# x in transposed layout, the first products taken ahead of the norm with its factor put on their results, and dt kept on chip

## The chip, the cores and the metric

The kernel runs on one core of a Trainium2 chip. That core has five engines, each with an instruction queue of its own: PE (TensorE, matrix products), DVE (VectorE), ACT (ScalarE), POOL (GpSimd) and SP (SyncE, which here only issues DMAs; ACT issues some too). On chip there are SBUF (128 partitions) and PSUM (eight banks, into which PE writes). The metric is device time in microseconds (us), the median of several executions.

## The reference, cut to what matters

One layer, 512 tokens, d_model 2048, float32 throughout:

```python
h = rmsnorm(x, norm_w)              # x * rsqrt(mean(x*x) + 1e-6) * norm_w
u = h @ w_in                        # one input projection, its columns split into
z_ssm, xbc, dt_f, dt_b, q_a, kv_a, z_attn, g_ssm, g_attn = split(u)
xbc = silu(dwconv(xbc) + bias)      # depthwise, four taps along the tokens
dt = softplus(dt + dt_bias)         # per head and direction
y = ssd(xs, dt, A, B, C) + flip(ssd(flip ...)) + d_skip * xs     # four groups
y = group_rmsnorm(y * silu(z_ssm))
o = mla(q_a, kv_a) * silu(z_attn)   # 16 heads
x + ((y @ w_proj_ssm) * sigmoid(g_ssm) + (o @ w_proj_attn) * sigmoid(g_attn)) @ w_out
```

followed by a last rmsnorm. The norm's root, r = rsqrt(mean(x*x) + 1e-6), is one number per token, so (x * norm_w) @ w, multiplied by r token by token, is h @ w.

## The kernel before

**Precision.** Every large product is made of three matmuls: each operand is split into a high part (rounded to the type fp32r) and a low part (what the rounding left), and `mm3` (L167) issues high x high, high x low, low x high for one k-block of 128. One such group of three is a *step* here. A product of a 128-column weight tile with all 512 tokens has 16 steps (D = 16 k-blocks). Weights come from DRAM in halves of 8 k-blocks: `wchunk` (L157) loads one half (SP issues it), ACT casts it to its high part, DVE subtracts for the low part (tile names wraw, wh, wl, three buffers each).

**Order.** PE's order is the program's. DVE, ACT, POOL and SP are ordered by a scheduler that takes ready work by priority; weights are requested ahead of their place (`ahead`, `tc.high_priority`). Each engine then runs its queue strictly in order.

**Start (L198 to L243).** x lies in DRAM with tokens in rows. It is loaded in 8 pieces (`xt`, [128 tokens, 1024]). ACT squares each piece and sums it over the row; the root per token comes from a few one-column instructions on DVE (`small_rsqrt`, L183); DVE (or ACT) multiplies the rows by it; PE turns all of it with 64 transposes (`x_turn`, L225) into eight PSUM banks; `x_out` (L227) multiplies by norm_w and splits, into h_h on ACT and h_l on DVE. Only then does the first product start.

**First products.** In this order: dt (64 rows of dt and 64 of the rotary key, `dtp`); then, for SSD group 0, the tiles xbc 4 and 5 (B and C) and xbc 0 to 3 (`xbc_gen`: the product, `conv_silu` on DVE and ACT, result to DRAM as `xbc_d`). Between them `h_sums` (L705) adds h_h and h_l together again and forms sums and differences of quarters of h (S1 to S4), the operands of the Strassen products; S1, S2, S4 stay in SBUF, x21 and S3 go to DRAM. `dt_make` (L278) computes softplus as a polynomial on DVE and writes dt and dt * A to DRAM (`dt_d`, `da_d`).

**Gates.** Three products of 2048 x 2048 (`wz`, `wgs`, `wga`) with the tokens, each by Strassen's scheme in two column halves cp; a half is seven products P1, P5, P6, P2, P3, P7, P4 (`Strassen.pair`, L630). Weight sums are made by a second load that adds into the first (`w_more`) or on POOL and DVE. Functions may be hung behind a product of a half (`hooks`).

**SSD.** Group 0 begins with `dt_turn` (L305; four transposes of dt64, which was loaded back from `dt_d` at L815) and `dt_sums` (L313; running sums of dt * A by four 128x128 matmuls); then BT and CT (L890, L891, xbc 4 and 5 from DRAM), xs (L894), and so on through four groups. Attention and the last products follow.

The few lines that the steps below rest on:

```python
def mm3(out, wh, wl, xh, xl, start, stop):
    pe.matmul(out, wh, xh, start=start, stop=False)
    pe.matmul(out, wh, xl, start=False, stop=False)
    pe.matmul(out, wl, xh, start=False, stop=stop)
```

## Time and profile before

| | us |
|---|---|
| median of 3 runs | 2069.7 (2066.1 to 2075.88) |
| profiled execution, its own time | 2068.9 |
| profiled execution, span | 2066.8 |

The page shows busy time of each engine, the span in 40 slices, the DMA queues and the chain of waits. A row of the trace reads: start and duration in us, engine, line, operation, out<-in by the program's names, sizes; in square brackets the idle time of the engine ahead of it and what ended that. A row of the windows reads: the stretch and its length, then busy us and count for PE, PE's weight load, DVE, ACT, POOL, then the granted clock of PE as a share of full speed, the DMA engines' busy share, and GB/s. In grouped rows the number after the bar is the group's busy time, then the mean ns of one. What the rows show is told in the prediction, where they are used.

### The profile page before, as it was taken

Reading aid. Unit: us, or ns where it says so; the run is one execution under the profiler, and the core shown is the slowest. Engines: PE = TensorE matmul, PEld = TensorE weight load, DVE = VectorE, ACT = ScalarE, POOL = GpSimd, SP = SyncE. Lnnn points to the kernel's source line nnn. Section 1 sums busy time; section 2 is a strip of 40 time slices with the busy share of each in tenths; the row PEclk is TensorE's granted clock in tenths of the full one; section 3 lists DMA queues with packets and bytes.
Section 4 is the critical chain, followed back from the end, with each engine's and each line's share of the span. In section 5 each row is a group of like instructions: output and inputs, shape, how many; then the busy total and the mean of one; then the engine's idle time right before and its main releaser. Section 6 shows DMA issues by size and latency. Waiting matters only on the chain.

```text
span 2066.8 us, 24703 instructions
## 1 busy us (share of the span) xinstructions
PE 1970.5 (95%) x9074; PEld 1627.3 (79%) x9074; DVE 1463.1 (71%) x1946; ACT 959.3 (46%) x1344; POOL 315.9 (15%) x337
## 2 busy tenths in 40 slices
PE   6999999999989999899899999999998999999998
PEld 5888888888867877787788788788877787888886
DVE  7976676676659689788786666667576888776342
ACT  6444444444444545445555344444444444443232
POOL 0011010010042151332420001110010111100110
PEclk9999999999999999999999999999999999999999
DMA  5567657656556837677564857873376876865332
GB/s 195 168 173 197 182 121 187 194 124 171 144 171 186 243 120 191 225 211 219 166 182 150 240 166 185 217 199 96 85 213 251 294 245 250 268 227 168 104 120 82
DMA packets 166584, 378.56 MB, mean 183 GB/s; under 512 B 16000, under 2 KB 65280, under 8 KB 165888
## 3 DMA queue, kind: packets, MB, share of 16 engines
q1 hardware_dynamic: 104688, 238.33, 35.2%
q0 software_dynamic: 26944, 92.29, 20.5%
q10 hardware_dynamic: 34832, 46.38, 6.3%
q8 instruction: 71, 1.16, 0.2%
q14 instruction: 49, 0.40, 0.1%
HBM read 325.03 MB, written 98.04 MB: 205 GB/s over the span
## 4 chain that ended last, share of the span: by engine, by line
PE 69%; DVE 11%; DMA 9%; issue 6%; ACT 2%; POOL 1%; SPq 0%; ACTq 0%; DVEq 0%; POOLq 0%
PE P L563 10%; PE P L564 10%; PE P L562 10%; PE f L1485 3%; PE f L1486 3%; PE f L1484 3%; PE za L168 2%; PE za L169 2%; PE za L170 2%; PE xbc L168 2%; PE xbc L169 2%; PE xbc L170 2%; DVE wl L164 2%; DVE sum L995 1%; DMA wraw<-wps 1%
## 5 line engine op out<-in xcount | busy, mean ns | idle before, releaser
L433 DVE TENSOR_TENSOR wl<-X,wh 128x1024 fp32r<-128x1024 f32 x152 | 185.2, 1222 | 81.8 <-ACT wh L432 81.3
L432 ACT CAST wh<-X 128x1024 fp32r<-128x1024 f32 x152 | 159.6, 1053 | 160.0 <-PE P L564 134.6
L164 DVE TENSOR_TENSOR wl<-wraw,wh 128x1024 fp32r<-128x1024 f32 (+2 forms) x148 | 175.4, 1186 | 81.7 <-ACT wh L163 76.4
L163 ACT CAST wh<-wraw 128x1024 fp32r<-128x1024 f32 (+2 forms) x150 | 145.3, 969 | 157.4 <-PE xbc L169 43.5
L433 DVE TENSOR_TENSOR wl<-wraw,wh 128x1024 fp32r<-128x1024 f32 x74 | 91.3, 1233 | 98.5 <-ACT wh L432 98.3
L168 PE MATMUL xbc<-h_h,wh 128*128 128x512 f32 x384 | 151.8, 395 | 0.0
L170 PE MATMUL xbc<-h_h,wl 128*128 128x512 f32 x384 | 150.2, 391 | 0.1
L169 PE MATMUL xbc<-h_l,wh 128*128 128x512 f32 x384 | 150.0, 391 | 0.0
L433 DVE TENSOR_TENSOR wl<-Y,wh 128x1024 fp32r<-128x1024 f32 x80 | 97.8, 1223 | 73.1 <-ACT wh L432 73.0
L563 PE MATMUL P<-wl,h_h 128*128 128x512 f32 x384 | 149.4, 389 | 0.0
L564 PE MATMUL P<-wh,h_l 128*128 128x512 f32 x384 | 149.4, 389 | 0.0
L562 PE MATMUL P<-wh,h_h 128*128 128x512 f32 x384 | 149.4, 389 | 0.0
L432 ACT CAST wh<-wraw 128x1024 fp32r<-128x1024 f32 x74 | 78.0, 1054 | 146.0 <-PE f L1486 71.0
L432 ACT CAST wh<-Y 128x1024 fp32r<-128x1024 f32 x80 | 84.2, 1053 | 114.8 <-PE P L564 95.3
L563 PE MATMUL P<-wl,S 128*128 128x512 f32 x288 | 112.4, 390 | 0.6 <-DVE wl L433 0.6
L564 PE MATMUL P<-wh,S 128*128 128x512 f32 x288 | 112.1, 389 | 0.0
L562 PE MATMUL P<-wh,S 128*128 128x512 f32 x288 | 112.1, 389 | 0.0
L170 PE MATMUL za<-h_h,wl 128*128 128x512 f32 x256 | 101.2, 395 | 5.0 <-DVE wl L164 5.0
L168 PE MATMUL za<-h_h,wh 128*128 128x512 f32 x256 | 102.3, 400 | 0.0
L169 PE MATMUL za<-h_l,wh 128*128 128x512 f32 x256 | 100.6, 393 | 0.0
L170 PEld LDWEIGHTS xbc<-h_h,wl 128*128 128x128 f32 x384 | 72.3, 188 | 16.1 <-DVE small L841 0.6
L168 PEld LDWEIGHTS xbc<-h_h,wh 128*128 128x128 f32 x384 | 72.6, 189 | 15.0 <-issue 0.2
(634 smaller groups left out, 5189.0 us busy)
## 6 DMA issues: line engine op xcount, KB each, us to landing
wraw<-wi SPq DMA_DIRECT2D x102, 512.0 KB, 4.1
da<-da_d SPq DMA_DIRECT2D x64, 256.0 KB, 4.4
T_wps<-wps POOLq DMA_DIRECT2D x32, 512.0 KB, 6.2
T_wpa<-wpa POOLq DMA_DIRECT2D x32, 512.0 KB, 9.9
wraw<-wo SPq DMA_DIRECT2D x32, 512.0 KB, 3.4
wraw<-wps SPq DMA_DIRECT2D x24, 512.0 KB, 5.0
xbc_d<-xbc ACTq DMA_DIRECT2D x24, 256.0 KB, 2.9
wraw<-wun SPq DMA_DIRECT2D x16, 384.0 KB, 3.1
```

Source lines behind the costliest of these rows:

```text
L163: act.copy(h, raw)
L164: (dve if ahead[0] else pool).tensor_sub(l, raw, h.bitcast(F32))
L168: pe.matmul(out, wh, xh, start=start, stop=False)
L169: pe.matmul(out, wh, xl, start=False, stop=False)
L170: pe.matmul(out, wl, xh, start=False, stop=stop)
L432: act.copy(hi_, raw)
L433: dve.tensor_sub(lo_, raw, hi_.bitcast(F32))
L562: pe.matmul(bs[i], xh, wh, start=(j == 0), stop=False)
L563: pe.matmul(bs[i], xh, wl, start=False, stop=False)
L564: pe.matmul(bs[i], xl, wh, start=False, stop=(j == 7))
L1484: pe.matmul(acc, mh, wh, start=(start and k == 0), stop=False)
L1485: pe.matmul(acc, mh, wl, start=False, stop=False)
```

## The change

**x comes transposed.** The host gives x a second time as `xt`, with the model dimension on the partitions: 8 pieces of [128, 1024], two k-blocks each. PE's 64 transposes go. SP loads the first halves of the weights of dt, xbc 4 and xbc 5 between the pieces. For each piece ACT squares it (`sq`), DVE multiplies it by norm_w (`x_t`, kept), and `x_split` makes h_h and h_l of it: the operands lack the root.

**Sums of squares** are now over the partitions: `square_sums(j)` takes the piece's squares as the stationary operand against one column of ones, 8 matmuls of one column for a piece, into four PSUM banks `ss`. `factor` makes the root of it (four tokens' columns at once), spreads it over a diagonal (`dg`), and four matmuls with ones give the root as a row for all partitions, which ACT copies to `R` [128, 512].

**Three products run at once.** dt, xbc 4 and xbc 5 are taken step by step in turns as `order` lists them (A, B, C), on operands without the root; the sums of squares stand after every second step and the factor after step 17. Their results are then multiplied by R. Meanwhile DVE multiplies x_t by R and splits it again, so that all that follows has h as before. xbc 0 and 1 run in turns too. `h_sums` takes its quarters from x_t, without adding h_h and h_l; it stands ahead of xbc 2 and xbc 3.

**dt.** The product's result (with bias) goes to DRAM (`dv_d`) and back; `dt_make` is hung behind P5 of the first gate's second half; dt64 stays in SBUF and `dt_d` is gone.

**The first gate** has its P1 and P2 of both halves taken ahead (`head`, `head_end`), as another product of the program had; its weight sums are made by second loads (16 more of 512 KB) and xbc 3 no longer stands between its first columns and its products.

The core of the diff:

```diff
+    for j in range(8):
+        xs = x_t[:, 2 * j:2 * j + 2, :].rearrange("p k t -> p (k t)")
+        nc.sync.dma_start(xs, a["xt"][j])
+        if j in (0, 1, 3):
+            early.append(wchunk(a["wi"][(T_DT, T_XBC + 4, T_XBC + 5)[len(early)], 0], 1024))
+        squares.append(sxq("sq"))
+        act.activation(squares[j], xs, AF.Square)
+        for k in (2 * j, 2 * j + 1):
+            dve.tensor_scalar_mul(x_t[:, k, :], x_t[:, k, :], vec[:, V_NORM + k:V_NORM + k + 1])
+            x_split(k)
...
+    def square_sums(j):
+        for k in range(2):
+            for t in range(TT):
+                pe.matmul(ss[t][:, 0:1], squares[j][:, k * SEQ + t * P:k * SEQ + (t + 1) * P], ones[:, 0:1],
+                          start=(j + k == 0), stop=(j == 7 and k == 1))
+    def factor():
+        v4 = few(4)
         for t in range(TT):
+            dve.tensor_scalar(v4[:, t:t + 1], ss[t][:, 0:1], 1.0 / D, EPS, ALU.mult, ALU.add)
+        r4 = small_rsqrt(v4, 4, lambda n: few(4))
+        dg = sx.tile([P, SEQ], F32, tag="v", bufs=1, name="dg")
+        for t in range(TT):
+            dve.tensor_scalar_mul(dg[:, t * P:(t + 1) * P], ident, r4[:, t:t + 1])
+        rp = pc("rp")
+        for t in range(TT):
+            pe.matmul(rp[:, t * P:(t + 1) * P], ones, dg[:, t * P:(t + 1) * P], start=True, stop=True)
+        act.copy(R, rp)
...
-        put(dt_d, dt64)
...
-        def columns(self, t, cp, m):
+        def columns(self, t, cp, m, headed):
             if self.made:
                 return t_load(t, self.w, cp, "T1", m)
-            return w_load(t, self.w, cp, 0, 0, m)
+            w_load(t, self.w, cp, 0, 0, m)
+            if headed:
+                w_more(t, self.w, cp, 0, 1, m, LOAD_AHEAD)
+            return t
...
+    order = "AABABABC" + "ABC" * 3 + "A" + "BCBC" + "ACAC" + "BABAC" + "ABC" * 3 + "A" + "BCBCBCC"
+    square_sums(0)
+    square_sums(1)
+    for i in together([gemm_steps(p_, win(t), h_h, h_l, w_) for p_, t, w_ in zip(firsts, (T_DT, T_XBC + 4, T_XBC + 5), early)], order):
+        if i % 2 == 1 and i // 2 < 6:
+            square_sums(2 + i // 2)
+        if i == 16:
+            factor()
+    v_ = sx.tile([P, SEQ], F32, tag="v", bufs=1, name="dt_v")
+    dve.tensor_mul(v_, firsts[0], R)
...
+    for k in range(KT):
+        dve.tensor_mul(x_t[:, k, :], x_t[:, k, :], R)
+        x_split(k)
+        if k in (1, 3):
+            xbc_done(4 + k // 2, firsts[1 + k // 2])
+    for i in together([xbc_gen(0, i, None) for i in (0, 1)], "AAA" + "AB" * 13 + "BBB"):
+        pass
+    for i in (2, 3):
+        h_sums(i - 2)
+        run(xbc_gen(0, i, None))
...
+    gates[0].hooks = {(0, "P5"): [lambda: h_ops.load("S3"), lambda: [h_part("S3", 256, q) for q in range(2)]],
+                      (1, "P5"): [dt_make]}
...
-    gates[0].first_columns(0)
-    run(xbc_gen(0, 3, None))
-    for p_ in gates:
+    run(gates[0].head())
+    run(gates[0].pair(0, True))
+    run(gates[0].head_end())
+    run(gates[0].pair(1, True))
+    for p_ in gates[1:]:
...
-    dt64 = tmp2("dt64")
-    with tc.high_priority(offset=LOAD_AHEAD):
-        nc.sync.dma_start(dt64, dt_d)
```

Three places of the instruction queues follow. In the rows, a name left of the arrow is the tile written, "x3" counts like instructions in a run.

PE's first instructions; before, the transposes (mm, pa, pb, pc are the eight banks, xt_239 and xt_256 two blocks of 128 tokens):

```order
L225 MATMUL mm<-cst,xt_239 128x128 x3
L225 MATMUL pa<-cst,xt_239 128x128 x2
L225 MATMUL pb<-cst,xt_239 128x128 x2
L225 MATMUL pc<-cst,xt_239 128x128
L225 MATMUL mm<-cst,xt_256 128x128 x3
```

and now, PE's first instructions, the sums of squares (ss) and the first two steps of the dt product:

```order
L236 MATMUL ss<-cst,sq 128x1 x16
L168 MATMUL dtp<-h_h,wh 128x512
L169 MATMUL dtp<-h_l,wh 128x512
L170 MATMUL dtp<-h_h,wl 128x512
L168 MATMUL dtp<-h_h,wh 128x512
L169 MATMUL dtp<-h_l,wh 128x512
L170 MATMUL dtp<-h_h,wl 128x512
L236 MATMUL ss<-cst,sq 128x1 x8
L168 MATMUL xbc<-h_h,wh 128x512
```

The products thus stand among the sums of squares at the head of the queue, and each waits for its own k-block alone.

DVE around the factor, now: the last scalings and subtractions of x (x_t, h_l), the root (small), the diagonal (dg), and then the first k-blocks times R:

```order
L228 TENSOR_SCALAR x_t<-x_t,vec 128x512 x5
L216 TENSOR_TENSOR h_l<-x_t,h_h 128x512 x5
L243 TENSOR_SCALAR small<-ss 128x1 x4
L187 RECIPROCAL small<-small 128x4
L188 TENSOR_TENSOR small<-small 128x4
L189 TENSOR_TENSOR small<-small 128x4
L190 TENSOR_SCALAR small<-small 128x4
L191 TENSOR_TENSOR small<-small 128x4
L247 TENSOR_SCALAR dg<-cst,small 128x128 x4
L753 TENSOR_TENSOR x_t<-x_t,R 128x512 x2
L164 TENSOR_TENSOR wl<-wraw,wh 128x1024
L216 TENSOR_TENSOR h_l<-x_t,h_h 128x512 x2
```

Before, the root stood there four times, once for each block of tokens, between scalings of rows; it stands there once now, behind all of x, and x's multiplication by R and second split come behind it.

SP where the gates end and the SSD begins; before, with dt's load ahead of BT and CT:

```order
L160 DMA wraw<-wi 128x1024 x3
L768 DMA Y<-h_x_199 128x1024 x2
L160 DMA wraw<-wi 128x1024 x3
L815 DMA dt_4305<-dt_d 128x512
L890 DMA BT<-xbc_d_4_97 128x512
L891 DMA CT<-xbc_d_5_98 128x512
L894 DMA xs<-xbc_d_0_93 128x512
```

and now:

```order
L160 DMA wraw<-wi 128x1024 x3
L794 DMA Y<-h_x_198 128x1024 x2
L160 DMA wraw<-wi 128x1024 x3
L916 DMA BT<-xbc_d_4_97 128x512
L917 DMA CT<-xbc_d_5_98 128x512
L920 DMA xs<-xbc_d_0_93 128x512
L920 DMA xs<-xbc_d_1_94 128x512
```

The load of dt has gone from the queue and nothing else at that place has moved.

More of the change, by code (lines that the diff above doesn't have):

```diff
@@ new lines, in build @@
+    squares, early = [], []
+    ahead[0] = 1
+    for j in range(8):
[8 more added lines that the diff above has]
+            x_split(k)
@@ L264, in build @@
-    for _ in range(5):
-        sxq("first")
-    def put(dst, t):
-        act.dma_start(dst, t)
-    dtp = in_gemm(T_DT, "dtp")
     ahead[0] = AHEAD
     da_d = dr.tile([64, SEQ], F32, name="da_d")
-    dv_, dt64 = sxd("dv_"), sxd("dt64")
-    act.activation(dv_[0:64, :], dtp[0:64, :], AF.Identity, bias=vec[0:64, V_DTB:V_DTB + 1])
-    act.copy(dv_[64:128, :], dtp[64:128, :])
-    put(kr_d, dv_[64:128, :])
-    def dt_make(new):
-        v = dv_[0:64, :]
-        e, u, pl, da64 = (new(n)[0:64, :] for n in ("e", "u", "pl", "da64"))
+    dv_d = dr.tile([64, SEQ], F32, name="dv_d")
@@ L367, in run, with gemm_steps @@
             pass
-    def gemm_steps(out, chunks, xh, xl):
+    def gemm_steps(out, chunks, xh, xl, first=None):
         total = sum(c[2] for c in chunks)
         for src, k0, nk in chunks:
-            h, l = wchunk(src, nk * P)
+            h, l = first if first and k0 == 0 else wchunk(src, nk * P)
             for k in range(nk):
@@ L626, in head, with head_end @@
             self.p1 = (a, b)
[L627 removed]
+        def head_end(self):
+            return self.second(1, self.p1[1], lambda i: sum_tile("p5"), None, "P2b")
         def pair(self, cp, headed=False):
@@ L730, in h_sums @@
-        keep("S4", x12)
-    for i in range(5):
-        run(xbc_gen(0, (4, 5, 0, 1, 2, 3)[i], sxt))
-        if i in (1, 3):
-            h_sums(i // 2)
-    dt_make(sxd)
+        s1, s3 = sxq("s1"), sxq("s3")
+        put(view4(h_d["x21"][:, cs]), x(1, 0))
+        dve.tensor_sub(view4(s1), x(1, 0), x(1, 1))
+        keep("S1", s1)
+        dve.tensor_sub(view4(s3), x(0, 0), x(1, 0))
+        put(h_d["S3"][:, cs], s3)
+        s2 = sxq("s2")
+        dve.tensor_sub(view4(s2), view4(s1), x(0, 0))
@@ new lines, in h_sums, with together, xbc_done @@
+        keep("S2", s2)
+        dve.tensor_add(view4(s1), view4(s2), x(0, 1))
+        keep("S4", s1)
+    def together(gens, order):
+        gens = {n: g_ for n, g_ in zip("ABC", gens)}
+        for i, n in enumerate(order):
+            next(gens[n])
+            yield i
+        for g_ in gens.values():
+            run(g_)
+    def xbc_done(i, p_):
+        v_ = sx.tile([P, SEQ], F32, tag="v", bufs=1, name="xbc_v")
+        dve.tensor_mul(v_, p_, R)
+        o = st("xbc")
+        put(xbc_d[0][i], conv_silu(v_, (4 + 12, 4 + 16)[i - 4], o, lambda n: o))
@@ new lines, in build @@
+    firsts = [mm(n) for n in ("dtp", "xbc", "xbc")]
+    order = "AABABABC" + "ABC" * 3 + "A" + "BCBC" + "ACAC" + "BABAC" + "ABC" * 3 + "A" + "BCBCBCC"
+    assert all(order.count(n) == KT for n in "ABC")
+    square_sums(0)
[5 more added lines that the diff above has]
+            factor()
```

118 lines of the change are left out of this document (43 added, 75 removed).

## Prediction, made before the changed kernel ran

> **What bounds the kernel now.** I read the page first: shares of busy time, the slices, the chain of waits.
>
> ```profile
> span 2066.8 us, 24703 instructions
> PE 1970.5 (95%) x9074; PEld 1627.3 (79%) x9074; DVE 1463.1 (71%) x1946; ACT 959.3 (46%) x1344; POOL 315.9 (15%) x337
> PE   6999999999989999899899999999998999999998
> PE 69%; DVE 11%; DMA 9%; issue 6%; ACT 2%; POOL 1%; SPq 0%; ACTq 0%; DVEq 0%; POOLq 0%
> ```
>
> PE is the bound, busy 95% of the span; only some 96 us can be won by waiting less. The first slice (a 6) is one of the few weak ones. Next, busy time by stretches up to the end of the gate products, and who PE waited for, here (the last of these rows is for 36 to 300 us alone):
>
> ```profile
> 0.00:36.00 36.00, 16.66 (x79) 13.54 (x80) 22.40 (x50) 25.39 (x43) 4.99 (x8) 1.00 0.54 203
> 36.00:300.00 264.00, 263.44 (x1160) 217.17 (x1159) 202.28 (x204) 123.78 (x139) 17.44 (x20) 1.00 0.61 168
> 300.00:566.00 266.00, 266.00 (x1175) 220.30 (x1174) 179.61 (x175) 128.71 (x143) 24.19 (x28) 1.00 0.63 164
> ...
> PE mm L225 <- DVE xt L220: 19.3, 4, 11.1
> PE pb L308 <- DMA dt<-dt_d: 5.4, 1, 5.4
> PE P L563 <- DVE wl L433: 0.6, 2, 0.3
> ```
>
> The first number after the stretch's length is PE's busy time. From 36 to 566 us PE stands still for 0.56 us in all. So the change can win in three places only: before the first product, those 0.6 us, and the 5.4 us on dt. The start, row by row on PE:
>
> ```profile
> 11.07 0.90 PE L225 MATMUL mm<-cst,xt 128*128 128x128 f32 x3 [11.07 <-DVE xt L220]
> ...
> 25.17 0.90 PE L225 MATMUL mm<-cst,xt 128*128 128x128 f32 x3 [6.30 <-DVE xt L220]
> ...
> 27.21 2.43 PE L225 MATMUL mm<-cst,xt 128*128 128x128 f32 x12
> 29.48 1.04 PE L225 MATMUL pa<-cst,xt 128*128 128x128 f32 x8
> ...
> 32.47 0.50 PE L168 MATMUL dtp<-h_h,wh 128*128 128x512 f32 x1
> ...
> 65.02 0.39 PE L170 MATMUL xbc<-h_h,wl 128*128 128x512 f32 x1
> 65.25 0.39 PE L168 MATMUL xbc<-h_h,wh 128*128 128x512 f32 x1
> ```
>
> The first product begins at 32.47; the first three (dt, xbc 4, xbc 5: 144 matmuls) end at 65.25, so a matmul takes 32.78 / 144 = 0.2276 us and a step of one product (three matmuls) 0.683 us. **65.25 is the mark that the new start has to beat.**
>
> **The change, part by part. 1: the start.** Removed are 64 transposes and the wait for the norm; PE now gets, while x comes in, 17 steps of the three products, 64 matmuls of one column (sums of squares) and the four of the factor; the other 31 steps follow it. When each can start is in these rows:
>
> ```profile
> 5.87 1.06 ACT L210 ACTIVATE scr<-xt 128x1024 f32<-128x1024 f32 x1 [2.71 <-DMA xt<-x]
> 7.50 1.06 ACT L210 ACTIVATE scr<-xt 128x1024 f32<-128x1024 f32 x1 [0.48 <-DMA xt<-x]
> 7.73 0.17 DVE L820 TENSOR_SCALAR small<-vec 128x8 f32<-128x8 f32 x1 [7.73 <-DMA vec<-vec]
> 8.68 0.16 DVE L212 TENSOR_TENSOR small<-small 128x1 f32<-128x1 f32 x1 [0.78 <-ACT scr L210]
> ...
> 10.07 0.16 DVE L191 TENSOR_TENSOR small<-small 128x1 f32<-128x1 f32 x1
> ...
> GB/s 0 33 195 280 309 394 426 393 418 422 410 430 414 422 422 414 426 401 37 0 0 0 90 262 209 250 238 0 0 0 0 0 0 0 16 0 0 0 82 356
> ...
> 75.25 0.41 DVE L286 TENSOR_SCALAR u<-e 64x512 f32<-64x512 f32 x1
> L595 DVE TENSOR_TENSOR u<-u,P 128x512 f32<-128x512 f32 x12 | 7.7, 680 | 0.0
> L433 DVE TENSOR_TENSOR wl<-wraw,wh 128x1024 fp32r<-128x1024 f32 x74 | 91.3, 1233 | 98.5 <-ACT wh L432 98.3
> L931 ACT CAST xw_h<-xw 128x512 fp32r<-128x512 f32 x24 | 14.8, 618 | 9.7 <-POOL xw L928 7.9 <-PE off L169 1.6 <-ACT y L851 0.2
> ```
>
> The first transfer was there at 5.87 and the second at 7.50; now a weight chunk is first and x's first piece second, so the first square ends near 8.5. The transfers (GB/s, 1 us a slice) move 0.41 MB a us: x (4.2 MB), three weight chunks (1.6) and the constants (0.5) are down by about 18 us, as the same bytes were before, and hide behind what follows. DVE, from 7.9: 16 scalings by norm_w at 0.41 (the row has 64 partitions; I take 512 elements to cost the same on 128), 16 subtractions at 0.68, three weight splits at 1.23 = 21.1, to 29.0. ACT, from 5.9: 8 squares at 1.06, 16 casts at 0.62, three of weights at 1.06 like the squares = 21.6, to 27.5, waits aside. The factor then costs DVE nine small instructions and four of 128x128 and ACT one root, some 3.2 us (the seven small ones and a root of before took from 8.68 to 10.23), and PE 0.9: **33.1 us by DVE**.
>
> By PE's queue it depends on the one-column matmul, which no row shows. The nearest, and what the clock does:
>
> ```profile
> 1126.96 1.00 PE L1016 MATMUL yb<-xT,G 128*128 128x64 f32 x8
> L1016 PE MATMUL yb<-xT,G 128*128 128x64 f32 x256 | 33.7, 277 | 1.0 <-DVE y L1019 1.0
> 576.85 1.12 PE L308 MATMUL pb<-cst,dt 128*128 128x128 f32 x4 [5.41 <-DMA dt<-dt_d]
> L308 PE MATMUL pb<-cst,dt 128*128 128x128 f32 x4 | 1.1, 436 | 5.4 <-DMA dt<-dt_d 5.4
> ...
> 574.00:578.00 4.00, 1.12 (x4) 0.72 (x4) 0.00 (x0) 0.00 (x0) 0.00 (x0) 0.66 0.78 272
> 578.00:582.00 4.00, 3.29 (x13) 3.01 (x14) 0.49 (x2) 3.41 (x6) 1.80 (x2) 0.50 1.08 379
> 582.00:586.00 4.00, 3.03 (x22) 2.44 (x21) 0.69 (x1) 2.67 (x6) 0.00 (x0) 0.99 0.77 263
> ```
>
> A true f32 matmul is two records: four matmuls of 64 columns are the eight of the first row, and with the last one's 0.277 taken off one begins every (1.00 - 0.277) / 7 = 0.104 us. Two passes of 64 columns, at a dense matmul's pace of 0.2276 / 4 for 128, are 0.057 of it, so about 0.047 is left for loading weights: a record of one column costs between 0.047 and 0.104. I take 0.07, about the middle. PE, from 8.5: 17 x 0.683 = 11.6, 128 x 0.07 = 9.0, eight of the factor 0.9; to 30.0. The clock column (third from the end) tells the rest: after a stall it fell to 0.50 for nearly 7 us and came back some 5 us into new work. At the start, too, 12 transposes took 2.43 us and the next ones, at 29.48, half of that each. So PE begins at half speed; 5 us of that cost 2.5, and the wait for the second square 1.1: **33.6 us by PE**, a near tie. With the tie not quite free I take 33.8; then 31 x 0.683 = 21.2: the three products end at 55.0. **Term 1: -10.2** (-11.5 with the best overlap on DVE, -5.9 with records at 0.104).
>
> On the clock, the Trainium skill ("TensorE: Matmul & The Clock Gate", Part 1) says that about 3.4 us of sustained matmul activity open it and an idle window of that length closes it; the rows above agree in size. Its Part 4 says that transposes don't count as such work. By that, the old start would have met its products cold; the halved transposes at 29.48 speak against it here. Whether one-column matmuls count is the first rival.
>
> **2: the same products' results, and x times the factor.** ACT's copy of R waits for PE, and behind it in ACT's queue stand the second weight halves, for which PE comes 3.4 us later: cast 1.05 and split 1.23 behind two multiplications, about 2.4 us after R, which fits. Then DVE multiplies x by R and splits it again (32 x 0.68 = 21.8), 11 weight splits (13.5), 18 convolution steps (13.2), the operand sums (8 x 1.23) and their splits (6 x 1.23), three results (2.0): 67.7 us, against 21.2 + 4 x 10.9 = 64.9 of PE until the next stage. DVE is full, as it was (a convolution step's row, and 30 to 105 us):
>
> ```profile
> L388 DVE SCALAR_TENSOR_TENSOR cacc<-xbc,vec,cacc 128x510 f32<-128x510 f32 x23 | 16.8, 732 | 0.0
> ...
> 30.00:105.00 75.00, 75.00 (x337) 61.61 (x336) 71.41 (x82) 38.67 (x48) 0.00 (x0) 1.00 0.50 161
> ```
>
> There DVE was 95% busy and PE lost nothing; what is late may slip into the four products after it, which need DVE for four splits (4.9 us) in 10.9. The tight point is the second weight half of xbc 1, behind S1's difference and the late splits of x. **Term 2: +1.5** (0 to +4).
>
> **3: dt on chip.** PE's 5.4 us on dt go; late next are BT and CT, which were in the same queue right behind:
>
> ```profile
> CT<-xbc_d SPq DMA_DIRECT2D x1, 256.0 KB, 7.4
> ...
> 578.59 0.62 ACT L895 CAST c_h<-CT 128x512 fp32r<-128x512 f32 x1
> ...
> 585.54 0.59 ACT L883 COPY xT<-pb 128x512 f32<-128x512 f32 x1 [0.26 <-PE pb L872]
> ...
> 586.20 2.04 POOL L928 TENSOR_TENSOR xw<-xT,wst 128x512 f32<-128x512 f32 x2 [5.10 <-ACT xT L883]
> ```
>
> CT was down at about 578.5; one 256 KB transfer fewer ahead puts it at 578.0. From there ACT does in order c_h 0.62, a table load 1.28, two exponentials, b_h and four xT, about 5.5 us: 583.5 in place of 586.1, and POOL's xw, on which PE's next product waits, follows. **Term 3: -2.6** (0 to -4.4). The dt arithmetic goes into the first gate's second half; it issues one load on SP, behind S3's two, and two writes on ACT, read 400 us later; in 36 to 300 us DVE is 77% busy.
>
> **4: the first gate's head.** Same seven products a half; 16 more loads of 512 KB (8.4 MB) in some 150 us, 56 GB/s on top of 168 at a DMA share of 0.61. POOL's accumulations now come four products early; they covered the 0.6 us. **Term 4: -0.6** (0 to -0.6). From the second gate on, each engine's order is as before but for dt's load.
>
> Sum: -10.2 + 1.5 - 2.6 - 0.6 = -11.9. The profiled execution took 2068.9 (2066.8 of span), 0.8 below the median of the runs shown; **2057.0**. The likeliest case alone spans 2053 to 2061.
>
> **The rivals.** *The clock stays half* (slower): if PE's short, load-heavy work doesn't open it, the stage to the factor runs at the half-clock price. At dt's row (four in 1.12 us, one every (1.12 - 0.436) / 3 = 0.228): 8.5 + 128 x 0.228 + 17 x 1.366 + 8 x 0.228 = 62.7, then 21.2 + 2.5: 86.4, or 21.2 late: 2068.9 + 21.2 + 1.5 - 3.2 = 2088. At half that price, 0.114, 2074. A us at half clock costs half a us: it decides if the clock opens later than about 37 us, 24 us after the time I allow. For it: waits between short matmuls. Against: transposes, half load, opened it. 0.12, half of it beyond 0.5%.
>
> *Dear weight loads*: a record at 0.104, as in the 64-column row, adds 128 x 0.034 = 4.4: 2061. 0.13. The same page ("LDWEIGHTS") gives columns / 1.2 ns, 107 ns for 128; with its floor of 25 ns an estimate of 0.132 a record, 7.9 us more, 2065. The trace speaks against that: 0.104 a record with the 64 columns in it.
>
> *DVE bounds the second stage*: 4 to 6 us at the tight point, 2061. 0.10. For it: 67.7 against 64.9.
>
> *It doesn't get ahead*: squares, scalings, casts and subtractions of a piece hand over between ACT and DVE; wholly in series a piece takes 4.5 us, the weights 6.9 in all, and the three products end 10 us past the mark (2077); half so, 2067. Both queues take two pieces in turn, which speaks against. 0.05.
>
> **The numbers.** 0.60 for the forecast. The range 2052 to 2066 leaves out the half clock, the last rival and a little below: 0.2. 0.5% (10.3 us) is about what a measurement of this kernel tells from no change: it lies at 2058.6, inside my case. Faster: 0.8 of 0.60 and a little of the rest, 0.51; slower 0.07; within 0.42.
>
> **What would show it.** The third product's end at 55, not 65.25; a one-column record at 0.07; the clock open by 15 us; PE's waits between 55 and 100 under 2 us, for wl of xbc; no wait on dt, and POOL's first xw 2.6 us earlier against the last gate product. A half clock to 35 us or a record over 0.10 breaks term 1.

## The result, and the profile after

The changed kernel took 2082.51 us (median of 16 runs, 2075.72 to 2091.96) against 2070.19 for the kernel before on the same chip (16 runs, 2062.41 to 2075.88): a ratio of the means of 1.007, 95% interval 1.0056 to 1.0084. **It is slower by 0.7%**; 2057 had been forecast. The profiled execution took 2075.72, the fastest of the 16, and 6.8 more than the one of before. From its page (the span, busy time of the engines):

```profile
span 2073.9 us, 24926 instructions
PE 1978.6 (95%) x9146; PEld 1635.9 (79%) x9146; DVE 1471.8 (71%) x1970; ACT 964.6 (47%) x1348; POOL 311.1 (15%) x335
```

PE was busy for 8.1 us more (1978.6 for 1970.5), although 64 transposes went. Where the time went is read from marks in PE's rows; a stage ends where the next matmul starts. Each kernel was profiled a second time in a later run, for the spread:

| us from the span's start | before | before, again | after | after, again |
|---|---|---|---|---|
| the first three products end | 65.25 | 65.19 | 64.50 | 61.3 |
| the gates begin | 108.77 | 108.71 | 108.09 | 104.89 |
| the last gate product ends | 567.20 | 566.66 | 576.52 | 572.84 |
| first SSD product (`loc`) | 589.45 | 590.39 | 599.02 | 595.65 |
| last SSD product (`yb`) | 1127.7 | 1138.4 | 1140.4 | 1143.5 |
| span | 2066.8 | 2075.1 | 2073.9 | 2079.5 |

The start won 0.75 (in the repeat 3.9), not 10; the gates lost 10.0 (468.4 for 458.4; 468.0 and 458.0 in the repeats); the way from the last gate product to the first SSD product stayed (22.25 and 23.7 before, 22.5 and 22.8 after). From there on the products are the same, and each kernel has a shorter and a longer execution of that stretch (538 and 548 us before, 541 and 548 after). The windows of the two longer ones follow, first the kernel before, again:

```profile
590.00:1139.00 549.00, 517.62 (x2398) 425.48 (x2397) 450.76 (x610) 279.21 (x413) 163.03 (x132) 0.97 0.63 182
```

and the changed kernel, again:

```profile
595.00:1144.00 549.00, 517.60 (x2398) 425.54 (x2397) 451.81 (x610) 279.33 (x413) 163.89 (x132) 0.97 0.63 182
```

PE's busy time agrees to 0.02 us, and the granted clock is 0.97 in both. So single profiles of one kernel differ by 7 to 10 us from this stretch alone, and the comparison has to be made at the marks.

**The start.** PE's rows of the changed kernel, from its first matmul on (`ss` are the one-column matmuls, two records each):

```profile
8.72 6.98 PE L236 MATMUL ss<-cst,sq 128*128 128x1 f32 x32 [8.72 <-ACT sq L226]
15.57 0.78 PE L168 MATMUL dtp<-h_h,wh 128*128 128x512 f32 x1
...
18.27 3.41 PE L236 MATMUL ss<-cst,sq 128*128 128x1 f32 x16
...
24.25 2.19 PE L236 MATMUL ss<-cst,sq 128*128 128x1 f32 x16
...
27.77 1.84 PE L236 MATMUL ss<-cst,sq 128*128 128x1 f32 x16
...
64.50 0.39 PE L168 MATMUL xbc<-h_h,wh 128*128 128x512 f32 x1
```

Sixteen records take 3.41 us at first and 1.84 later. From one start to the next it is 0.213 at half clock and, at full clock, (1.84 - 0.14) / 16 = 0.1065. The row at 24.25 lies between: the clock opened near 25, that is, it went from half to full. Between 8.72 and 64.50 PE has no idle time at all; it was slow, not late. (The windows' clock column gives 1.00 for this stretch; the durations show the half clock.)

**The gates.** First the stretches of the changed kernel, then PE's waits from 36 to 300 us (us in total, times, longest):

```profile
36.00:108.00 72.00, 72.00 (x330) 59.91 (x330) 64.33 (x90) 37.94 (x50) 0.00 (x0) 1.00 0.43 140
108.00:152.00 44.00, 40.04 (x172) 31.42 (x171) 24.43 (x24) 23.00 (x28) 3.61 (x4) 1.00 0.96 318
210.00:222.00 12.00, 8.02 (x28) 6.14 (x27) 10.92 (x9) 2.77 (x4) 0.00 (x0) 0.86 0.43 125
222.00:566.00 344.00, 344.00 (x1519) 284.95 (x1518) 245.62 (x246) 164.16 (x183) 31.10 (x36) 1.00 0.63 166
```

```profile
PE P L552 <- DVE wl L422: 6.0, 3, 4.0
PE P1b L552 <- DVE wl L422: 1.1, 2, 0.8
PE P1b L551 <- ACT wh L421: 0.8, 1, 0.8
```

PE loses 4.0 between 133 and 149 us and 4.0 at 216. For the first, see DVE's last split of `h_sums`, and SP's weight loads and its first request for X (weights of the first gate's sums), in the timeline of the changed kernel:

```profile
104.02 1.21 DVE L422 TENSOR_TENSOR S<-s,S 128x1024 fp32r<-128x1024 f32 x1
86.53 17.26 SPq L452 DMA_DIRECT2D wraw<-wz  x4
105.29 0.33 SPq L452 DMA_DIRECT2D X<-wz  x1
```

and its stretches about that time:

```profile
96.00:108.00 12.00, 12.00 (x55) 9.94 (x54) 10.33 (x11) 5.58 (x7) 0.00 (x0) 1.00 0.52 168
108.00:148.00 40.00, 37.05 (x159) 29.11 (x157) 20.43 (x20) 19.68 (x23) 3.61 (x4) 1.00 1.01 335
```

and the same two views of the kernel before, the request first:

```profile
95.33 3.40 SPq L463 DMA_DIRECT2D X<-wz  x4
```

```profile
96.00:108.00 12.00, 12.00 (x55) 9.93 (x54) 9.62 (x12) 5.92 (x7) 0.71 (x1) 1.00 1.01 325
108.00:140.00 32.00, 31.44 (x137) 25.04 (x136) 23.75 (x22) 14.71 (x17) 2.93 (x4) 1.00 0.56 153
```

X is requested 0.06 us after the last split of `h_sums` ends (104.02 + 1.21), ten us later than before. But that split is only the last thing it waits for: SP's queue reaches X only at 103.8 (86.53 + 17.26), since the fourth of the weight loads ahead of it had waited 9.0 us, until 103.47, for a buffer that another of DVE's splits frees; the split of `h_sums` adds 1.4. Both are work of a full DVE. Before, the transfers filled the DMA engines ahead of the gate (share 1.01 from 96 to 108); now that stretch is half empty and the next 40 us run at 1.01, with second loads of the head among them. That the short waits of 133 to 149 us come from this crowd is read from the shares; the runs below test its parts. For the second loss, DVE's rows around 212 us:

```profile
211.05 0.42 DVE L273 TENSOR_SCALAR p<-e 64x512 f32<-64x512 f32 x1 [2.72 <-DMA zs_d<-p]
211.50 3.34 DVE L274 RECIPROCAL p<-p 64x512 f32<-64x512 f32 x1
214.77 2.28 DVE L422 TENSOR_TENSOR wl<-X,wh 128x1024 fp32r<-128x1024 f32 x2
```

The arithmetic of dt waits 2.72 us for a buffer that is still being written out, its reciprocal takes 3.34, and the split that PE needs stands behind both. The clock then falls for 3.4 us (0.86 over the stretch of 210 to 222), worth 1.7 more.

**The start of SSD.** PE's rows of the changed kernel, SP's loads, the cast behind them on ACT, and last SP's load of dt in the kernel before:

```profile
586.23 0.63 PE L898 MATMUL pb<-cst,BT 128*128 128x128 f32 x4 [2.69 <-DMA BT<-xbc_d]
590.29 1.11 PE L898 MATMUL pb<-cst,xs 128*128 128x128 f32 x4 [3.43 <-ACT dec L310]
...
576.34 3.05 SPq L160 DMA_DIRECT2D wraw<-wi  x2
579.48 0.41 SPq L916 DMA_DIRECT2D BT<-xbc_d  x1
579.98 0.42 SPq L917 DMA_DIRECT2D CT<-xbc_d  x1
...
587.43 0.62 ACT L921 CAST c_h<-CT 128x512 fp32r<-128x512 f32 x1 [5.54 <-DMA CT<-xbc_d]
...
570.16 0.41 SPq L815 DMA_DIRECT2D dt<-dt_d  x1
```

The wait on dt is gone (5.4) and two stand in its place (6.1): one for BT, one for ACT's copy `dec`, which stands behind the cast of CT. BT is issued 3.0 us after the last gate product (576.52), as dt was before (570.16 against 567.20), since it stands in SP's queue behind the same weight loads.

### The profile page after: what moved, and what is told of

It is laid out like the page before. It is cut to its first block, busy times and chain, and to the rows that moved or that the text cites. A ratio compares the mean times of both kernels' runs of the same rounds, so it can differ in the third digit from the quotient of the medians.

```text
span 2073.9 us, 24926 instructions
## 1 busy us (share of the span) xinstructions
PE 1978.6 (95%) x9146; PEld 1635.9 (79%) x9146; DVE 1471.8 (71%) x1970; ACT 964.6 (47%) x1348; POOL 311.1 (15%) x335
## 4 chain that ended last, share of the span: by engine, by line
PE 72%; DVE 10%; DMA 9%; issue 6%; ACT 2%; POOL 1%; SPq 0%; ACTq 0%; DVEq 0%; POOLq 0%
PE P L552 9%; PE P L553 9%; PE P L551 9%; PE f L1515 3%; PE f L1516 3%; PE f L1514 3%; PE xbc L168 2%; PE xbc L169 2%; PE xbc L170 2%; PE za L168 2%; PE za L170 2%; PE za L169 2%; DVE wl L422 2%; DVE wl L164 2%; DMA wraw<-wps 1%
## 5 line engine op out<-in xcount | busy, mean ns | idle before, releaser
L422 DVE TENSOR_TENSOR wl<-X,wh 128x1024 fp32r<-128x1024 f32 x144 | 175.3, 1222 | 64.2 <-ACT wh L421 63.4
L421 ACT CAST wh<-X 128x1024 fp32r<-128x1024 f32 x144 | 151.1, 1053 | 144.0 <-PE P L553 123.7
L422 DVE TENSOR_TENSOR wl<-wraw,wh 128x1024 fp32r<-128x1024 f32 x82 | 101.3, 1235 | 119.7 <-ACT wh L421 119.5
L421 ACT CAST wh<-wraw 128x1024 fp32r<-128x1024 f32 x82 | 86.4, 1053 | 160.5 <-PE f L1516 70.8
L552 PE MATMUL P<-wl,h_h 128*128 128x512 f32 x352 | 137.0, 389 | 0.0
L551 PE MATMUL P<-wh,h_h 128*128 128x512 f32 x352 | 137.0, 389 | 0.0
L553 PE MATMUL P<-wh,h_l 128*128 128x512 f32 x352 | 137.0, 389 | 0.0
L169 PEld LDWEIGHTS xbc<-h_l,wh 128*128 128x128 f32 x384 | 72.9, 190 | 15.0 <-issue 0.2
```

The lines of the kernel that those rows point to most:

```text
L421: act.copy(hi_, raw)
L422: dve.tensor_sub(lo_, raw, hi_.bitcast(F32))
L551: pe.matmul(bs[i], xh, wh, start=(j == 0), stop=False)
L552: pe.matmul(bs[i], xh, wl, start=False, stop=False)
L553: pe.matmul(bs[i], xl, wh, start=False, stop=(j == 7))
```

## The experiments

Each result is the median in us, then the ratio to the kernel before, run beside it, with its 95% interval. Where no base is named, the edit is to the changed kernel. The diffs show the lines that matter; `...` stands for lines left out.

**The first gate as before.**

```diff
-    run(gates[0].head())
-    run(gates[0].pair(0, True))
-    run(gates[0].head_end())
-    run(gates[0].pair(1, True))
-    for p_ in gates[1:]:
+    for p_ in gates:
```

> The changed kernel with its first gate taken as before (no P1 and P2 ahead, no second weight loads; xbc 3 still ahead of the gates, dt's arithmetic still hung behind P5 of the second half). From PE's first gate product to its first product behind the gates the changed kernel took 468.4 us and before took 458.4. Theory A (the head's second loads fill the DMA engines between 116 and 148 us and starve the splits; dt's arithmetic makes the other 5.7 us): the four short waits of 133 to 149 us (4.0 us) go; 460 to 464, by where the scheduler now puts dt's reciprocal; the kernel 4 to 9 us faster than the changed one. Rival (DVE's backlog from the second stage, full from 50 to 100 us, reaches into the gates): waits of 3 to 4 us stay in 108 to 150, phase above 465, gain under 2 us.

2082.19; 1.006 [1.0042, 1.0078]. The gates took 464.4 (468.4 with the head), but 5.3 us of waits stayed in them, X was requested at 106.0, and the median gained nothing that it resolves. The head explains a part; the late request is there without it. Here X, which lies where `h_sums` has its scratch, waits 3.7 us for the last split of `h_sums`; ahead of it in SP's queue stands a load of S3 (`xraw`), issued at 101.47.

**dt's arithmetic in the second gate.**

```diff
-                      (1, "P5"): [dt_make]}
...
+    gates[1].hooks = {(0, "P3"): [dt_make]}
```

> The changed kernel with dt's arithmetic hung behind P3 of the second gate's first half in place of P5 of the first gate's second half. Theory A (dt's reciprocal, 3.34 us, and the wait for its tile's store, 2.7 us, stand in DVE's queue ahead of the split that PE waits for at 212 us, and the pause halves the clock for 3.4 us): the wait of 4.0 us and the half clock behind it go; the gates take about 462.7 us (468.4 less 5.7); 5 to 6 us faster than the changed kernel. Rival (the wait is for the accumulating second loads, dt's arithmetic only stands near it): a wait of 3 us or more stays at the border of the two halves, no gain.

2081.26; 1.007 [1.0045, 1.0095]. The wait at 216 and its half clock are gone (gates 465.9), 2.0 us of new ones come at 327 to 331. That dt's arithmetic made the wait is shown; moving it won 2.5 us in the profile and nothing that the median resolves.

**The squares summed on POOL**, so that 16 records are left of 128.

```diff
+        if j:
+            pool.tensor_add(squares[j], squares[j], squares[j - 1])
...
-    square_sums(0)
-    square_sums(1)
...
+        if i == 11:
+            square_sums(7)
```

> The changed kernel with the eight squared pieces added up on POOL, so that PE has 16 one-column records (8 matmuls) in place of 128. Theory A (the start is bound by PE: 128 records of 0.107 us, 0.214 while the clock is half, and one-column work does not open the clock): PE's first step begins near 11, the clock opens by 15 to 21 in place of 25, the three products end at 49 to 53 in place of 64.5; then DVE binds the second stage, waits of 2 to 6 us for xbc's wl, so that the gates begin 8 to 13 us earlier than 108.1. Rival B (the start is bound by the squares, casts and subtractions on ACT and DVE, PE only fills the time): the three products end above 60. Rival C (the clock opens by time since the start and not by the kind of work): open at 25 still, end at 53 to 55.

2088.07; 1.0091 [1.0073, 1.0108]: worse. The three products ended at 69.2, not at 49 to 53. POOL's first addition, and DVE's scalings before and beside it:

```profile
11.16 2.38 POOL L228 TENSOR_TENSOR sq<-sq 128x1024 f32<-128x1024 f32 x1 [10.28 <-ACT sq L226]
...
8.48 0.87 DVE L230 TENSOR_SCALAR x_t<-x_t,vec 128x512 f32<-128x512 f32 x2
...
11.12 3.10 DVE L230 TENSOR_SCALAR x_t<-x_t,vec 128x512 f32<-128x512 f32 x2 [0.19 <-ACT sq L226]
```

Two scalings take 3.10 in place of 0.87: one of them stood still for the length of POOL's instruction. The Trainium skill ("SBUF — State Buffer", Who interferes with whom) states that DVE, in some modes and operations, and GpSimd (POOL) contend for a shared port pair under a lock that one holds for a whole instruction; this trace agrees, 2.23 us more beside a 2.38 us addition.

**PE warmed ahead of the sums** by four f32 matmuls of 512 columns on zeroes.

```diff
+    pool.memset(R, 0.0)
+    wm = pc("wm")
+    for _ in range(4):
+        pe.matmul(wm, R[:, :P], R, start=True, stop=True)
```

> The changed kernel with four f32 matmuls of 512 columns on a zeroed tile put ahead of PE's first work, from about 1.5 to 9.5 us (their result is read by nobody). Theory A (PE runs at half clock until dense work has filled a stretch of some 3.4 us, which costs 8 us of the 16 from 8.7 to 25): the clock is open by 8 to 12 us, a one-column record takes 0.107 from then on, the three products end at 56 to 59 in place of 64.5; 5 to 8 us faster than the changed kernel. Rival C (the clock opens at a set time after the start): records of 0.214 until 25, end at 64.5 or a little later, no gain. Rival B (ACT and DVE bind the start): clock open, but PE waits for sq and h_l, end above 62.

2082.54; 1.0062 [1.0043, 1.008]. Stretches from 8 us on:

```profile
8.00:11.00 3.00, 2.08 (x17) 1.86 (x16) 2.71 (x5) 2.09 (x4) 0.00 (x0) 1.00 1.02 419
11.00:18.00 7.00, 6.48 (x26) 5.90 (x26) 6.76 (x13) 7.00 (x11) 0.00 (x0) 0.51 1.03 420
18.00:22.00 4.00, 4.00 (x32) 3.75 (x31) 3.98 (x8) 3.72 (x6) 0.00 (x0) 1.00 0.85 323
```

and two of PE's rows there:

```profile
8.52 1.95 PE L240 MATMUL ss<-cst,sq 128*128 128x1 f32 x16 [0.39 <-ACT sq L230]
11.52 3.58 PE L240 MATMUL ss<-cst,sq 128*128 128x1 f32 x16 [1.06 <-ACT sq L230]
```

The clock was open when the sums began (16 records in 1.95) and fell to half at 11, when PE had run nothing but these sums for 2.5 us, with 1.45 of idle time around them. It stayed there through the next 16 and opened at 18, after six 512-column matmuls from 14.96 on. Whether the idle time or the one-column work closed it isn't told apart here; whether such work can open it, the run with more of it, below, shows. The products ended at 60.8, 3.7 earlier than in the changed kernel's first profile and 0.5 earlier than in its second; the median gained nothing that it resolves.

**Dense sums**: the squares, rounded to fp32r, go against a matrix of ones, 16 matmuls of 512 columns in place of 64 of one column.

```diff
-            for t in range(TT):
-                pe.matmul(ss[t][:, 0:1], squares[j][:, k * SEQ + t * P:k * SEQ + (t + 1) * P], ones[:, 0:1],
-                          start=(j + k == 0), stop=(j == 7 and k == 1))
+            pe.matmul(total, one_r, squares[j][:, k * SEQ:(k + 1) * SEQ], start=(j + k == 0), stop=(j == 7 and k == 1))
...
```

> The changed kernel with the sums of squares made by dense matmuls: ACT writes the squares as fp32r, 16 matmuls of 512 columns against a block of ones add them up (3.6 us at full clock in place of 13.7), ACT copies the sum (the same row on every partition) and four one-column matmuls turn it onto the token partitions; the rest of the factor is as it was. Theory A (one-column records are dear and count as idle for the clock): the clock is open by 14 to 19 us, the three products end at 49 to 54 in place of 61 to 67, the gates begin at 95 to 103, with DVE as the bound in between; the median 6 to 14 us below the changed kernel's 2082.5, and the spread of its runs is smaller since the clock's opening is no longer a matter of chance. Rival B (ACT and DVE bind the start): three products end above 60. Rival C (clock opens at a set time): open at 25 or later.

2072.37; 1.0018 [1.0001, 1.0035]. The products end at 54.86. That this is within 0.2 us of the mark of the prediction is chance: PE does other work here than was summed there. PE at the first sums, and at the factor:

```profile
7.97 1.22 PE L237 MATMUL total<-sq,one_r 128*128 128x512 f32 x2 [7.97 <-ACT sq L226]
14.33 0.63 PE L237 MATMUL total<-sq,one_r 128*128 128x512 f32 x2
31.24 2.08 PE L254 MATMUL rp<-dg,cst 128*128 128x128 f32 x8 [1.83 <-DVE dg L251]
```

Two take 1.22 and at 14.33 half of it: the clock is open by then, not at 25. Stopping at the factor costs 1.83 and half clock until 34.4. The start now wins 10 us, but the gates take 465.7, and the median is 0.2% above that of the kernel before.

**64 more one-column records ahead of the sums.**

```diff
+    ex_ = pc("more")
+    for t in range(4 * 8):
+        pe.matmul(ex_[:, 0:1], squares[0][:, t % 8 * P:(t % 8 + 1) * P], ones[:, 0:1], start=True, stop=True)
```

> The changed kernel with 32 one-column matmuls more (64 records) ahead of PE's first ones, results read by nobody. Theory A (one-column work, however back to back, does not open the clock): PE is busy from 8.7 on with one-column records alone, for 96 x 0.214 = 20.5 us, six stretches of 3.4 us, and stays at half clock through all of them and some 9 us into the mix with products; open at 35 or later, the three products end 10 to 16 us later than in the changed kernel (61 to 67). Rival (any busy stretch opens the clock): open by 18, records of 0.107 from then on, the three products end less than 8 us later.

2088.95 (one run). PE's rows:

```profile
8.62 13.81 PE L740 MATMUL more<-cst,sq 128*128 128x1 f32 x64 [8.62 <-ACT sq L226]
22.30 6.97 PE L236 MATMUL ss<-cst,sq 128*128 128x1 f32 x32
29.12 0.77 PE L168 MATMUL dtp<-h_h,wh 128*128 128x512 f32 x1
...
35.29 1.84 PE L236 MATMUL ss<-cst,sq 128*128 128x1 f32 x16
```

20.5 us of nothing but one-column records, back to back, left the clock at half (0.213 each to the last); it opened some 3 us after the steps began at 29.12. **For opening the clock, such work counts as idle time here.** Whether it also closes an open clock, no run shows by itself. The Trainium skill ("TensorE: Matmul & The Clock Gate", Part 1) lets sustained matmul activity of about 3.4 us open the clock; with the 512-column steps that agrees, and for one-column matmuls, though PE's row counts them as busy, this run shows that it doesn't hold.

**dt kept on chip, alone**, in the kernel before.

```diff
+    dt64 = gp.tile([P, SEQ], F32, tag="st", bufs=3, name="dt64")
...
-        put(dt_d, dt64)
...
-    dt64 = tmp2("dt64")
-    with tc.high_priority(offset=LOAD_AHEAD):
-        nc.sync.dma_start(dt64, dt_d)
```

> The kernel before with dt kept on chip as the only change: dt64 stays in SBUF, its store and load go. Theory A (BT and CT, next in SP's queue, take dt's place and land as late as dt did, and the fill of the first group is as it was): from the last gate product to the first product of the states (loc) 21 to 22.5 us, as before (22.2), the kernel within 2 us of before. The prediction's step (CT lands 0.5 us earlier and everything behind it 2.6 us): 19 to 20 us, the kernel 2 to 3 us faster.

2081.54; 1.0064 [1.0042, 1.0086]: this part alone is slower, too. PE at the start of SSD:

```profile
582.07 0.63 PE L869 MATMUL pb<-cst,BT 128*128 128x128 f32 x4 [2.11 <-DMA BT<-xbc_d]
586.74 1.11 PE L869 MATMUL pb<-cst,xs 128*128 128x128 f32 x4 [4.04 <-ACT dec L321]
```

The wait of 5.4 became 2.1 and 4.0, and from the last gate product to the first SSD product it takes 23.4 us (22.25 and 23.7 before). The first gate also waits 3.1 us at 112, its X requested at 106.56 in place of 95.33, behind three weight loads that SP's queue issues from 95.26 on. What dt64, which holds a buffer for longer there, has to do with that was not tried.

**The two kernels again**, for a second profile of each.

> The changed kernel once more, for a second profile of it. Theory A: the clock opens anywhere between 18 and 50 us, by how the stretches of 3.4 us fall on the one-column blocks; each us of delay costs half a us, so that the end of the three products lies between 61 and 77; the gates take 466 to 471 us. Rival (the spread of the runs is made later): the three products end within 1 us of 64.5.

> The kernel before once more, for a second profile of it. If the changed kernels lose in the SSD by more than chance (538.2 us from the first product of the states to the last yb in the first profile of before, 539.5 to 548.7 in the changed ones, 17 us at half clock against 17 to 37), this shows 537 to 540 and 17 us; if that is chance alone, any value from 538 to 549 may come.

2081.3 and 2077.08 (one run each); their marks are in the table above.

**The first gate's early loads through the other ring**, without the head.

```diff
+            early = self is gates[0] and cp == 0
...
+            elif early:
+                p1 = evict((yield from self.first(0, "P1")), "p1")
...
```

> The changed kernel with its first gate taken as before, but for P1 of its first half, whose weights come through the ring wraw (4 extra loads of 512 KB in place of 16), so that they need not wait for the place under x_t. Theory A (two things cost in the first gate: with the head, the DMA engines are full from 108 to 148 us; without it, X waits for the place that x_t holds until about 105 us, 10 us later than before; and dt's reciprocal in front of a split that PE waits for): neither is there, and the scheduler puts the reciprocal among Y's splits; waits in the gates under 2 us in all, gates 458.5 to 461 us (468.2 in the changed kernel, 458.4 before), the median 5 to 10 us below the changed kernel's 2082.5. Rival (DVE's backlog from the second stage is what the first gate waits for): waits of 3 us or more stay in 108 to 140.

2080.78; 1.0053 [1.0035, 1.0072]. A miss: X is requested at 104.95, PE waits 4.78 for it at 124, with half clock behind it, and the gates take 468.2.

**Dense sums, the factor's matmuls six steps later, and the edit above.**

> Dense sums of squares (as in e5), the factor's four matmuls six steps behind its sums, so that PE does not wait for them, and the first gate as in e9. Theory A: the three products end at 51 to 54, the gates begin at 95 to 98 and take 458.5 to 462; from the start to the first product of the states 11 to 14 us less than before (589.45); median 2057 to 2064 where before has 2067 to 2070. Rival (what the runs behind the profile lose lies in the SSD and attention, whatever the start): the lead of the start is there in the profile, but the median is within 4 us of before.

2067.1; 0.9989 [0.9976, 1.0003], above the 2057 to 2064 expected. The products end at 51.3, so the factor's stop is gone; PE waits 5.35 at 112 instead, and the gates take 467.9.

**dt's transposes and sums right after the gates** in that kernel, with the split of CT put behind those of BT and xs.

> e10 with dt turned and summed right at the end of the gates, ahead of the filling products, and 14 filling steps (9.6 us) in place of six between that and the transposes of BT. Theory A (with dt on chip nothing of it needs to wait, but BT and CT land some 10 us behind the last gate product, and the six steps ahead of dt cover 4 of them): PE's waits on BT and on dec (2.7 and 3.4 us in the changed kernel) go but for 1 to 2 us, and the clock stays open or loses one stretch: 4 to 7 us less than e10. Rival (POOL's xw and the copies behind BT are the chain; PE's order does not matter): the wait moves to the first product of the states, gain under 2 us.

2068.78; 1.0002 [0.9986, 1.0017]. The rival was right: PE waits 4.1 for `daT` (the copy of dt's transposes) and 4.0 for `xw_h` (an operand of the first SSD product) instead.

**h_sums on POOL**, so that X is asked for earlier: with the gate as before, then with dense sums as well.

```diff
-        dve.tensor_sub(view4(s1), x(1, 0), x(1, 1))
+        pool.tensor_sub(view4(s1), x(1, 0), x(1, 1))
...
```

> The kernel of e1 (first gate as before, no head) with the eight sums and differences of h_sums on POOL in place of DVE. Theory D (what the first gate waits for is X's place: X lies where h_sums has its scratch, is requested when the last split of S4 is done, at 105 to 106 us in the changed kernels against 95.3 in before, and DVE, full since 44 us, is why that is late): 9.8 us of DVE's 61 go to POOL, X is requested at 95 to 100, the waits of 111 to 137 us (5.0 us in e1) fall under 2 us, the gates take 459 to 461.5 us (464.4 in e1). Rival (POOL's adds, 2.4 us each against 1.22, make a longer chain than DVE's backlog): X is requested at 104 or later, waits as in e1.

> e13 with the dense sums of squares and the later factor of e10. Theory D with A: the gates begin at 95 to 97 (108.7 in before), X is requested 8 us or more ahead of that, the gates take 459 to 461.5; the first product of the states at 577 to 581 (589.5 and 590.4 in before); median 2057 to 2063 where before has 2067 to 2070. Rival (X late all the same, since PE is earlier too): waits of 4 us or more at the first gate, median 2064 to 2068.

2091.5, 1.0105 [1.0079, 1.013], and 2081.05, 1.0053 [1.0037, 1.0068]. Both are misses: X was asked for at 103.93 and at 92.82, but the gates began only at 119.85 and 109.3. From the first, DVE and PE:

```profile
79.55 2.87 DVE L377 SCALAR_TENSOR_TENSOR xbc<-xbc_v,vec,xbc 128x510 f32<-128x510 f32 x1
88.27 0.79 PE L170 MATMUL xbc<-h_h,wl 128*128 128x512 f32 x1 [7.30 <-DVE wl L164]
```

Beside POOL a convolution step takes 2.87 for 0.74, and PE waits 7.3 us for a weight split of DVE, which has no idle time from 60 to 90 us.

**BT and CT issued by POOL**, in the last kernel.

```diff
-            nc.sync.dma_start(BT, xbc_d[g][4])
+            (nc.sync if g else pool).dma_start(BT, xbc_d[g][4])
```

> e14 with the loads of BT and CT of the first group issued by POOL's queue in place of SP's, where they stand behind a weight load that waits for its ring. Theory A (dt's place in SP's queue was taken by BT and CT, and that queue, not the transfer, makes them late): both land 2 to 4 us earlier against the last gate product, from there to the first product of the states 19 to 21 us in place of 23 to 24. Rival (the place of BT and CT comes free only then, or the engines are full): the same 23 to 24.

2074.91; 1.002 [1.0001, 1.0038]. From the last gate product to the first SSD product it takes 20.07 us, 22.15 without this edit; BT is asked for at 567.81, 10.8 us before the last gate product.

**Dense sums, later factor, the gate as before, BT and CT on POOL's queue.**

> Dense sums with the later factor (e10), the first gate wholly as before (e1), h_sums on DVE, and BT and CT of the first group on POOL's queue (e15). Theory D with A: the gates begin at 95 to 97, X is requested at 93 to 95 and so lands behind its need: short waits of 4 to 6 us in the first gate as in e1, none long enough to halve the clock, gates 463 to 465.5 (467.9 in e10); from the last gate product to the first product of the states 20 to 21 us (24.2 in e10); that product at 579 to 582 (589.5 and 590.4 in before); median 2058 to 2065, where before has 2068.6. Rival (the first gate's wait only moves): one wait of 4 us or more and a halved clock, gates 467 or more, median 2064 to 2068.

**2061.14; 0.9963 [0.9947, 0.9978], faster than both kernels.** The products end at 51.7, the gates take 464.2, and it is 16.04 to the first SSD product, where POOL and ACT show:

```profile
550.23 0.57 POOL L922 DMA_DIRECT2D BT<-xbc_d  x1 [15.46 <-DVE wl L430]
...
566.01 0.38 ACT L308 COPY daT<-pb 128x256 f32<-128x256 f32 x1
566.28 0.63 ACT L927 CAST c_h<-CT 128x512 fp32r<-128x512 f32 x1
```

BT is asked for 11 us before the last gate product (561.02), and CT's cast follows dt's copies at once. That the loads' place in SP's queue held the wait is shown by this and the run before.

**Fewer DVE instructions at the start** (norm_w folded into the cast, the split and the product with R), on that kernel.

> e16 with norm_w folded into the split (ACT casts with it as a scale, DVE subtracts and later multiplies by it and R in one instruction), so that DVE has 16 scalings of 0.41 us less. Theory D (X's request hangs on DVE, which is full from R to the end of h_sums): R is ready up to 2 us earlier, X is requested 2 to 5 us earlier than in e16 (93 to 95), the waits of the first gate fall by 1 to 3 us, the median by 1 to 4 us. Rival (PE's sums of squares and ACT set R; DVE's scalings lie beside them): X requested within 1 us of e16, the same time.

2066.56; 0.9983 [0.9968, 0.9998]. A miss: X is requested at 94.30, later than in that kernel (92.00), and the first gate waits 4.1 with half clock behind it.

**X placed behind the small tiles**, so that other buffers free it, on the kernel before that one (dense sums, BT and CT on POOL's queue).

```diff
-    for tag, n, w in (("X", 4, 1024), ("p1", 2, SEQ), ("p5", 2, SEQ), ("u", 2, SEQ), ("kk", 2, SEQ), ("Y", 4, 1024)):
+    for tag, n, w in (("p1", 2, SEQ), ("p5", 2, SEQ), ("u", 2, SEQ), ("kk", 2, SEQ), ("X", 4, 1024), ("Y", 4, 1024)):
```

> e16 with the tiles of the first gate's pool laid out in another order (p1, p5, u, kk ahead of X), so that X lies under x_t, which h_sums reads for the last time 3.6 us before its last split, and no longer under h_sums' scratch. Nothing else moves in any queue. Theory D (X's request waits for its place): X is requested at 88 to 89 against the same marks where e16 has 92.0 (gates beginning at 96.8 there), the waits in the first gate (5.4 us in e16) fall by 2 to 3.5 us, the median by 1 to 4 us. Rival (the engines are full with what else is asked for, or X's place is not what it waits for): X at 91 or later, or waits within 1 us of e16's.

2060.71; 0.9959 [0.9946, 0.9971], the lowest median, though not to be told from that of the kernel it edits (0.9963 [0.9947, 0.9978]). SP's request:

```profile
88.24 2.16 SPq L460 DMA_DIRECT2D X<-wz  x4
```

That is 3.8 us earlier, so the place does hold it there; PE's waits from 60 to 560 us went from 6.0 to 4.1. What the rest of these waits, 0.8 us at most each, come from is open.

## Why the prediction was wrong

Two terms carry the miss at the marks, about ten us each: the start and the first gate.

- **Term 1, the start (-10.2 forecast, -0.75 measured)**, is the step that failed first, in two sizes. "I take 0.07" for a one-column record: it is 0.1065, so 128 x 0.0365 = 4.7 more, and above even the upper end of 0.104. That is the rival of dear weight loads, given 0.13. The wrong step was to take 0.057 off the 64-column row for its columns: a record of one column takes as long as one of 64 (0.1065 and 0.104), and at half clock as long as dt's transposes with 128 (0.213 and 0.214), so in these rows the columns add nothing, which leaves the weight load. (The 0.104 is 0.103 when divided out, and dt's records start every 0.214, not 0.228; both change little.) The Trainium skill's 107 ns for a weight load ("TensorE: Matmul & The Clock Gate", LDWEIGHTS) agrees with 0.1065 alone, without the floor that I had put on top. And "5 us of that cost 2.5": the clock opened at 25, after 16.3 us at half, which cost 8.1, so 5.6 more. I had taken the halved transposes of before as a sign that light work opens the clock; for one-column matmuls the long run of them shows otherwise. With 0.2 for a later begin and 1.1 for a wait that didn't come: 55.0 + 4.7 + 5.6 + 0.2 - 1.1 = 64.4, measured 64.5. Both rivals were listed, each as the whole story; what happened is all of one and a part of the other. When the clock opens is partly luck: in the repeat it opened at 18.3, and the start won 3.9.
- **Term 2 (+1.5 forecast, +0.1 measured)**: no PE wait at all from 64.5 to 108. But "DVE is full" was right, and I priced it only where PE could wait at once. The price was paid in a transfer: the weight loads ahead of X wait for buffers that DVE frees, DVE's last split of `h_sums` ends at 105.2, and X is requested then.
- **Term 4 (-0.6 forecast, +10.0 measured)**, the costliest step that failed: the overlap of the 16 loads with the gate's other transfers, and dt's place in DVE's queue. The 16 loads were spread in the estimate over "some 150 us" on an average share of 0.61; they fell together with the late X in 40 us at 1.01. Waits of 4.0 there, 4.0 at dt's arithmetic and 1.7 of half clock, less the 0.6 of before, are 9.1 of the 10.0; 0.9 is not attributed. The part of dt's arithmetic is shown by moving it. Of the short waits ahead of it the runs show that the head alone doesn't make them (5.3 stay without it) and that X's place makes a part (6.0 became 4.1); no run of the changed kernel brought the gates back to the 458 of before (462.8 was the least), so the rest of this cause is argued, not shown. Of dt I had counted the DMAs and DVE's average load (77%), not that a wait for a buffer and a reciprocal of 3.34 us stand in DVE's queue in front of a split for PE.
- **Term 3 (-2.6 forecast, +0.3 measured)**: "one 256 KB transfer fewer ahead" moves nothing, since BT takes dt's slot behind weight loads that wait for their buffers. The queue, not the transfer, set the time: on another queue the way to the first SSD product fell from 22.15 to 20.07 by that edit alone, and to 16.04 in the kernel with dense sums.
- The rest: the two profiled executions differ by 6.8 us, the medians by 12.3. The profiled one of the changed kernel was lucky: it has the highest granted clock of the 16 (0.987). Over the 16 the clock is 0.9829 in the mean, over 114 executions of the kernel before beside the experiments 0.9847. Each us at half clock loses half a us, so an estimate of the loss is (1 - clock) x 2070, which is 35.4 against 31.7: 3.7 us more for the changed kernel. Where these lie is open: in the two profiles of each kernel, the way from the first SSD product to the end takes no more time in the changed one (1474.9 and 1483.9 us) than before (1477.4 and 1484.7).

## What to carry to other kernels

Work that PE shows as busy isn't always work that opens its clock: here a reduction by matmul was better made dense, against a matrix of ones, than with one column. Price a full off-path engine by what it releases, buffers and through them transfers, and look at the load on the DMA engines in the stretch where the requests will fall, not on the average. When a wait is removed, ask for the next one's place in its issue queue before counting a gain.

## What the hardware showed unexpectedly

- One-column f32 matmuls: 0.1065 us a record at full clock, 0.213 at half, no less than with 64 columns (0.104 at full clock); 20.5 us of them in a row didn't open the clock.
- One POOL addition of 2.4 to 3.2 us held a DVE instruction of 0.44 to 0.74 us back by 2.1 to 2.2 us, so moving additions to POOL made a full DVE later.
- The same stretch of SSD took 538 and 548 us in two executions of the kernel before, and 541 and 548 in two of the changed one.
